# Homes of 1280 bytes at one offset for the moving operands of a float32r GEMM chain

## The chip, the cores and the metric

The kernel runs on one core of one Trainium2 chip. The metric is the device time of one execution in microseconds, as the median of several runs. One execution is also recorded by the hardware profiler; its trace gives the start and length of the instructions on each engine. TensorE multiplies matrices: of a matmul's two operands, one (here 128x128 weights) is loaded into the array first, and the other, the moving operand, is streamed through it. VectorE (DVE), ScalarE (ACT) and GpSimd (POOL) work on elements, SyncE (SP) issues most of the transfers. SBUF is the memory on the core: 128 partitions, in each of which a tile occupies one contiguous stretch of bytes. "Home" stands below for such a stretch, an address in every partition that is the same for all of them.

## What is computed

One step of a hybrid decoder layer over 256 prompt tokens and 8 sample tokens, which the kernel treats as 264 columns. All sums are in float32.

```python
hx = rmsnorm(x, norm_mix)
proj = hx @ w_in                       # 2048 -> 11264
hc, bg, cg, q, fz, iv, og, ga, gb = split(proj)
a = bg * causal_conv3(cg * hc)         # short convolution branch
o, s_new = hgrn2(silu(q), 1 - f, iv, log f)      # 8 heads of 128, gated recurrence
o = rmsnorm(o, onorm_g) * silu(og)
mix = sigmoid(ga) * (a @ w_branch_a) + sigmoid(gb) * (o @ w_branch_b)
x = x + mix @ w_out
h2 = rmsnorm(x, norm_ffn)
x = x + square(relu(h2 @ w_up)) @ w_down         # 2048 -> 8192 -> 2048
y = rmsnorm(x, norm_final)
```

Outputs are y for both kinds of tokens and the new states of the convolution and the recurrence.

## The kernel before

Activations lie transposed: features in the partitions, the 264 tokens along them. A matrix of 2048 features is 16 tiles of 128x264, each 264 x 4 = 1056 bytes per partition. One GEMM makes 128 output features: it walks over 16 blocks k of 128 input features and adds up in one PSUM bank.

To keep float32's precision, each operand is split in two float32r parts, hi (the value rounded to float32r) and lo (the rest). `split` (L58) does it with a cast on ACT (L59) and a subtraction on DVE (L60). `gemm` (L84) then issues three matmuls for each k: weights hi with operand hi (L88), weights hi with operand lo (L89), weights lo with operand hi (L90). So a GEMM of 16 blocks is 48 matmuls of 128x264, and the moving operand changes hi, lo, hi within a block and steps to the next pair of homes for the next block.

Weights come in blocks of 1 MB (`fetch_w`, L65) through SP's queue into `wraw` (two buffers, four once `wraw2` is there), are split in halves (`split_w`, L72) into `whi` and `wlo` of 4096 bytes, four buffers each, and are read 512 bytes at a time.

The stages, in order:

1. Head (`hd`, L157 to L187). Four output blocks are computed together while x and the first weights arrive. For each k, the scaled x is split into `xgh` and `xgl` (L164, L165), which stay for all later GEMMs on x. Each pair (weights part, x part) is streamed against four weight blocks in turn (L179).
2. Projections and recurrence (L484 to L527), an order written out by hand: one weight block for each of 56 slots, GEMM `proj` on the `xg` tiles, the result scaled by `rstd1` out of PSUM. The heads' recurrence (`hgrn`, steps s0 to s14 in successive slots) and the convolution run on the other engines beside it, with small matmuls between GEMMs. Step s3 (L294) makes `kin`, s5 and s6 read it on TensorE; s8 (L367) makes `o`, which s9 to s12 read. The results are split into `oh`, `ol` (L403) and `ah`, `al` (L433), the branch operands.
3. Gates and branches (L542 to L562): for each of 16 output blocks, two gate GEMMs `proj` (fewer at the start) and two GEMMs `br..a`, `br..o` of 8 blocks on the branch operands; the mix is split into `mxh`, `mxl`.
4. `wo` (L567 to L587): 16 GEMMs on the `mx` tiles. The result plus x goes to `x2t` (L574), 4 tiles of four blocks; scaled and split, `x2h` and `x2l` take over the homes of the `xg` tiles.
5. Four quarters of `up` (16 GEMMs on `x2h`, `x2l`) and `dn` (16 GEMMs on `hh`, `hl`, which take the homes of the `mx` tiles), L592 to L630.
6. The end (L633 to L652): the last norm, five multiplications and six transfers of y. After that TensorE runs a probe (L644 to L652): 42 matmuls with float32r operands of 128 to 512 columns out of the last `whi` tile, and 6 in bf16, into a PSUM bank that nobody reads.

Memory comes from pools that are stacked from one end of SBUF: `const`, `wraw`, `wsp`, `act`, `tmp`, then, one after the other in the same place, `xp` and `hp` of the early stages, and `mx`, `x2p`, `wraw2` of the later ones. `act` holds 64 homes of 1056 bytes, 32 for the `xg` and 32 for the `ao` tag (branch operands); `mx` holds 32. In a stack of such homes every next one starts 1056 = 4 x 256 + 32 bytes further. A tag's homes are reused when their last reader is done; a later tile waits for that. Outside the two blocks in a hand-made order (L484 and L633), a scheduler orders the instructions and keeps these waits.

Of the kernel before, what the change touches and what calls it, by code (L numbers as in the profile page):

```python
# [8 lines left out]
F32 = mybir.dt.float32  # L9
F32R = mybir.dt.float32r  # L10
U32 = mybir.dt.uint32
BF16 = mybir.dt.bfloat16
AF = mybir.ActivationFunctionType
ALU = mybir.AluOpType
AX = mybir.AxisListType
# [25 lines left out]
def hybrid_step(ctx: ExitStack, tc: tile.TileContext, x, par, sconv, shg, w_hd, w_in, w_br, w_out, w_up, w_dn,  # L41
# [8 lines left out]
    wraw = ctx.enter_context(tc.tile_pool(name="wraw", bufs=2))  # L50
    wsp = ctx.enter_context(tc.tile_pool(name="wsp", bufs=4))
    act = ctx.enter_context(tc.tile_pool(name="act", bufs=32))
    tmp = ctx.enter_context(tc.tile_pool(name="tmp", bufs=9))
    acc = ctx.enter_context(tc.tile_pool(name="acc", bufs=5, space=PS))
    mps = ctx.enter_context(tc.tile_pool(name="mps", bufs=3, space=PS))
    dram = ctx.enter_context(tc.tile_pool(name="dram", bufs=1, space=bass.MemoryType.DRAM))

    def split(src, hi, lo):  # L58
        nc.scalar.copy(hi, src)  # L59
        nc.vector.tensor_tensor(lo, src, hi.bitcast(F32), op=ALU.subtract)  # L60

    raws = [wraw]
    last_hi = []

    def fetch_w(src):  # L65
        pool = raws.pop(0)
# [5 lines left out]
    def split_w(w, h):  # L72

        hi = wsp.tile([P, 8, P], F32R, tag="hi", name="whi")
        lo = wsp.tile([P, 8, P], F32R, tag="lo", name="wlo")
        split(w[:, h * 1024:(h + 1) * 1024].rearrange("p (k c) -> p k c", c=P), hi, lo)
        last_hi.append(hi)
        return [(hi[:, k], lo[:, k]) for k in range(8)]

    def load_w(src):  # L80
# [55 lines left out]

    pt = const.tile([P, N_PAR], F32, name="pt")
    xg = []
    ss1 = const.tile([P, T], F32, name="ss1")
    p0 = ExitStack()  # L140
    xp = p0.enter_context(tc.tile_pool(name="xp", bufs=1))
    xsq = xp.tile([P, 4, T], F32, name="xsq")
# [14 lines left out]
    for g in range(4):  # L157
        xt, w = xts[g], wts[g]
        whi = [wsp.tile([P, 2, 512], F32R, tag="hi", name="whi") for _ in range(2)]
        wlo = [wsp.tile([P, 2, 512], F32R, tag="lo", name="wlo") for _ in range(2)]  # L160
        for j in range(4):
            k = 4 * g + j
            gk = pt[:, C_NMIX + k:C_NMIX + k + 1]
            hi = act.tile([P, T], F32R, tag="xg", name=f"xgh{k}")  # L164
            lo = act.tile([P, T], F32R, tag="xg", name=f"xgl{k}")  # L165
            wh, wl = whi[j // 2][:, j % 2], wlo[j // 2][:, j % 2]
            if g == 0:
                (nc.vector.tensor_copy if k == 0 else nc.scalar.copy)(wh, w[:, j])
                nc.scalar.activation(hi, xt[:, j], AF.Copy, scale=gk)
                nc.vector.tensor_tensor(wl, w[:, j], wh.bitcast(F32), op=ALU.subtract)  # L170
            else:
                if j % 2 == 0:
                    split(w[:, j:j + 2], whi[j // 2], wlo[j // 2])
                nc.scalar.activation(hi, xt[:, j], AF.Copy, scale=gk)
            nc.vector.scalar_tensor_tensor(lo, xt[:, j], gk, hi.bitcast(F32), op0=ALU.mult, op1=ALU.subtract)
            xg.append((hi, lo))
            for a, b, st, sp in ((wh, hi, k == 0, False), (wl, hi, False, False), (wh, lo, False, k == NK - 1)):
                for i in range(4):
                    nc.tensor.matmul(hps[i], a[:, i * P:(i + 1) * P], b, start=st, stop=sp)  # L179
        if g == 0:  # L180
            nc.scalar.activation(xsq, xt, AF.Square)
        else:
            sq = xp.tile([P, 4, T], F32, tag="xsq2", name="sq", bufs=2)
            nc.scalar.activation(sq, xt, AF.Square)
            nc.vector.tensor_tensor(xsq, xsq, sq, op=ALU.add)
# [14 lines left out]
    nc.gpsimd.memset(smask.rearrange("p a (n l) -> p (a n) l", l=CH)[:, :, 0:1], 0.0)  # L200


    rstd1 = const.tile([P, T], F32, name="rstd1")
    ao = {}
    hctx = ExitStack()
    hp = hctx.enter_context(tc.tile_pool(name="hp", bufs=1))
# [16 lines left out]
    def hgrn(j, q, fz, iv, og):  # L223
# [61 lines left out]
        def s3():  # L285
            for i in range(2):
                fb = hp.tile([P, TS, P], F32, tag="fb", name="fb", bufs=2)
                qb = hp.tile([P, TS, P], F32, tag="qb", name="qb", bufs=2)
                so = hp.tile([P, TS, P], F32, tag="so", name="so", bufs=2)
                nc.sync.dma_start(so, shg[2 * j + i])  # L290
                nc.sync.dma_start(fb, st["scr"][0, i].partition_broadcast(P))
                nc.sync.dma_start(qb, st["scr"][1, i].partition_broadcast(P))
                st["s", i] = fb, qb, so
            st["eb"], st["kin"] = pair_tile("eb", w=TP), pair_tile("kin", w=TP)  # L294
            nc.scalar.activation(st["kend"], st["kend"], AF.Exp)
            nc.scalar.activation(st["kin"], st["b"], AF.Exp, scale=-1.0)
            nc.scalar.activation(st["eb"], st["b"], AF.Exp)
# [66 lines left out]
                                     start=False, stop=(n == 3))  # L364

        def s8():
            o = st["o"] = pair_tile("o")  # L367
            for i in range(2):
                nc.scalar.copy(o[:, i, :TP], st["ops", i][:, :TP])
            s_out(0)  # L370
            for i in range(2):
                nc.sync.dma_start(nhg_p[2 * j + i], st["S", i][:, 3])
# [27 lines left out]

        def s14():
            for i in range(2):
                hi = act.tile([P, T], F32R, tag="ao", name="oh")  # L403
                lo = act.tile([P, T], F32R, tag="ao", name="ol")
                split(og[:, i], hi, lo)
                ao["o", 2 * j + i] = (hi, lo)

# [22 lines left out]
        return a  # L430

    def conv_split(c, a):
        hi = act.tile([P, T], F32R, tag="ao", name="ah")  # L433
        lo = act.tile([P, T], F32R, tag="ao", name="al")
        split(a, hi, lo)
        ao["a", c] = (hi, lo)

# [98 lines left out]


    mx = ctx.enter_context(tc.tile_pool(name="mx", bufs=32))
    x2p = ctx.enter_context(tc.tile_pool(name="x2p", bufs=1))
    raws.append(ctx.enter_context(tc.tile_pool(name="wraw2", bufs=2)))  # L540
    x2t = [x2p.tile([P, 4, T], F32, name=f"x2t{g}") for g in range(4)]
    mix = []  # L542
    for m in range(NK):
        sg = []
        for base in (GA, GB):
            if m < 2:
                t = gate0.pop(0)
            else:
                t = t264("gate")
                proj(base + m, t)  # L550
            nc.scalar.activation(t, t, AF.Sigmoid)
            sg.append(t)
        wk = load_w(w_br[m])
        for i, n in enumerate(("a", "o")):
            ps = acc_tile(f"br{m}{n}")
            gemm(ps, wk[8 * i:8 * i + 8], [ao[n, c] for c in range(8)])
            nc.vector.tensor_tensor(sg[i], sg[i], ps, op=ALU.mult)
        nc.vector.tensor_tensor(sg[0], sg[0], sg[1], op=ALU.add)
        hi = mx.tile([P, T], F32R, tag="mx", name="mxh")
        lo = mx.tile([P, T], F32R, tag="mx", name="mxl")  # L560
        split(sg[0], hi, lo)
        mix.append((hi, lo))  # L562


    x2, x2g = [], []
    ss2 = const.tile([P, T], F32, name="ss2")
    for m in range(NK):  # L567
        xr = t264("xr")
        nc.sync.dma_start(xr, x[:, m, :])
# [3 lines left out]
        t = x2t[m // 4][:, m % 4]  # L573
        nc.vector.tensor_tensor(t, ps, xr, op=ALU.add)  # L574
        gk = pt[:, C_NFFN + m:C_NFFN + m + 1]
        hi = act.tile([P, T], F32R, tag="xg", name="x2h")
        lo = act.tile([P, T], F32R, tag="xg", name="x2l")
        nc.scalar.activation(hi, t, AF.Copy, scale=gk)
        nc.vector.scalar_tensor_tensor(lo, t, gk, hi.bitcast(F32), op0=ALU.mult, op1=ALU.subtract)
        if m == 0:  # L580
# [6 lines left out]
        x2g.append((hi, lo))  # L587


    ss3 = const.tile([P, T], F32, name="ss3")  # L590
    rstd2 = None
    for qd in range(NQ):  # L592
        hh = []
        for m in range(NK):
            wk = load_w(w_up[qd * NK + m])
            ps = acc_tile("up")
            gemm(ps, wk, x2g)
            if rstd2 is None:
                ps2 = mps.tile([P, 512], F32, tag="m", name="ps2")
                sumsq(ps2, ss2, True, True)  # L600
                rstd2 = const.tile([P, T], F32, name="rstd2")
                nc.scalar.copy(rstd2, rstd_bcast(rstd_diag(ps2, 2048, "rstd2"), "rstd2"))
            t = t264("h")
            nc.vector.scalar_tensor_tensor(t, ps, 0.0, rstd2, op0=ALU.max, op1=ALU.mult)
            nc.scalar.activation(t, t, AF.Square)
            hi = mx.tile([P, T], F32R, tag="mx", name="hh")
            lo = mx.tile([P, T], F32R, tag="mx", name="hl")
            split(t, hi, lo)
            hh.append((hi, lo))
        for m in range(NK):  # L610
# [22 lines left out]
    with tc.manual_schedule():  # L633
# [6 lines left out]
        nc.vector.scalar_tensor_tensor(x2[-1], x2[-1], pt[:, C_NFIN + 15:C_NFIN + 16], bps,  # L640
                                       op0=ALU.mult, op1=ALU.mult)
        nc.sync.dma_start(y[:, 15:16, :], x2t[3][:, 3:4])

        probe = acc.tile([P, 512], F32, tag="acc", name="probe")  # L644
        mv = last_hi[-1]
        row = mv.rearrange("p k c -> p (k c)")
        for n in (512, 128, 256, 264, 280, 320, 384):
            for k in range(6):
                nc.tensor.matmul(probe[:, :n], mv[:, k], row[:, :n], start=True, stop=True)  # L649
        half_w = row.bitcast(BF16)  # L650
        for k in range(6):
            nc.tensor.matmul(probe[:, :T], half_w[:, k * P:(k + 1) * P], half_w[:, :T], start=True, stop=True)  # L652


# [53 lines left out]
```

## Time and profile before

| | us |
|---|---|
| median of 3 runs | 1501.76 (1501.73 to 1501.98) |
| profiled execution | 1501.61 |
| its span, first to last instruction | 1499.9 |
| first `proj` matmul | 32.9 |
| first branch matmul | 387.1 |
| first `wo` matmul | 643.5 |
| first `up` matmul | 737.2 |
| last `dn` matmul | 1486.5 |

The first three rows come from the times, the others from the trace, in microseconds from the start of the span. The granted TensorE clock was 0.999 of full speed over the span. A page of the profile gives, for each group of instructions, line, engine, operation, output and inputs by the program's names, the count, busy time, mean duration, and idle time ahead of it with what ended it. The views of a tile give, for each line, minimum, median and maximum duration in ns, and first and last start. A row of the timeline gives start, length, engine, line and count; several instructions in a row that are alike are merged. Durations of matmuls overlap, so their distance is read from starts.

### The profile page before, as it was taken

To read this page: it belongs to the slowest core of one execution; us is meant where nothing else is said; L and a number is where in the kernel's file an instruction comes from. 1 tells how busy PE (TensorE), PEld (TensorE's weight loads), DVE (VectorE), ACT (ScalarE), POOL (GpSimd) and SP (SyncE) were. 2 spreads that over 40 slices of the span, in tenths; PEclk is the share of its full clock that TensorE was granted. 3 is DMA by queue.
4 is the path that set the end of the run, shared out by engine and by line. 5 is a ranking of instruction groups with operands and counts; after the bars stand their busy time and mean duration, and the time that the engine had idled before them with its cause. 6 is when DMAs were issued, how large, how long until landed. Compare 5 with 4: busy or idle time off the path is not lost.

```text
span 1499.9 us, 28243 instructions
## 1 busy us (share of the span) xinstructions
PE 1492.7 (100%) x12230; PEld 1487.2 (99%) x12230; DVE 884.8 (59%) x1154; ACT 705.8 (47%) x946; POOL 57.6 (4%) x86
## 2 busy tenths in 40 slices
PE   9999999999999999999999999999999999999999
PEld 8999999999999999999999999999999999999998
DVE  7576777777655555566655545555455554455554
ACT  6556565646444444444454433444334433344542
POOL 0001011012000000001100000000000000000000
PEclk9999999999999999999999999999999999999999
DMA  6565756665655454555545555454554545545441
GB/s 258 185 256 184 263 189 237 211 241 203 243 176 190 172 192 171 186 202 196 206 170 182 184 172 192 171 186 180 174 192 170 191 173 180 186 171 193 171 169 59
DMA packets 47501, 285.91 MB, mean 191 GB/s; under 512 B 5472, under 2 KB 9328, under 8 KB 16144
## 3 DMA queue, kind: packets, MB, share of 16 engines
q1 hardware_dynamic: 46560, 283.38, 53.0%
q8 instruction: 95, 1.56, 0.4%
q10 hardware_dynamic: 720, 0.59, 0.1%
q14 instruction: 30, 0.25, 0.0%
q0 software_dynamic: 96, 0.14, 0.0%
HBM read 277.07 MB, written 7.02 MB: 189 GB/s over the span
## 4 chain that ended last, share of the span: by engine, by line
PE 98%; DVE 1%; DMA 1%; ACT 0%; issue 0%; ACTq 0%
PE proj L88 11%; PE proj L89 11%; PE proj L90 10%; PE dn L88 8%; PE dn L90 8%; PE up L88 8%; PE dn L89 8%; PE up L89 8%; PE up L90 8%; PE wo L89 2%; PE wo L90 2%; PE wo L88 2%; PE hd L179 1%; PE probe L649 1%; DMA wt<-in_w_hd_dram 0%; PE dlps L332 0%
## 5 line engine op out<-in xcount | busy, mean ns | idle before, releaser
L59 ACT CAST whi<-w 128x1024 fp32r<-128x1024 f32 x488 | 509.5, 1050 | 696.8 <-PE dn L89 218.6
L60 DVE TENSOR_TENSOR wlo<-w,whi 128x1024 fp32r<-128x1024 f32 x488 | 597.8, 1234 | 371.3 <-ACT whi L59 369.5
L88 PE MATMUL proj<-xgh,whi 128*128 128x264 f32 x1344 | 383.5, 285 | 0.4 <-DVE q L462 0.4
L90 PE MATMUL proj<-xgh,wlo 128*128 128x264 f32 x1344 | 381.9, 284 | 0.0
L89 PE MATMUL proj<-xgl,whi 128*128 128x264 f32 x1344 | 380.9, 283 | 0.0
L88 PE MATMUL dn<-hh,whi 128*128 128x264 f32 x1024 | 292.7, 286 | 0.0
L90 PE MATMUL dn<-hh,wlo 128*128 128x264 f32 x1024 | 291.6, 285 | 0.0
L89 PE MATMUL dn<-hl,whi 128*128 128x264 f32 x1024 | 291.4, 285 | 0.0
L89 PE MATMUL up<-x2l,whi 128*128 128x264 f32 x1024 | 291.2, 284 | 0.0
L88 PE MATMUL up<-x2h,whi 128*128 128x264 f32 x1024 | 290.8, 284 | 0.0
L90 PE MATMUL up<-x2h,wlo 128*128 128x264 f32 x1024 | 289.7, 283 | 0.0
L88 PEld LDWEIGHTS proj<-xgh,whi 128*128 128x128 f32 x1344 | 253.4, 189 | 1.7 <-ACT whi L59 0.5
L89 PEld LDWEIGHTS proj<-xgl,whi 128*128 128x128 f32 x1344 | 253.4, 189 | 0.2
L90 PEld LDWEIGHTS proj<-xgh,wlo 128*128 128x128 f32 x1344 | 252.3, 188 | 0.0
L90 PEld LDWEIGHTS dn<-hh,wlo 128*128 128x128 f32 x1024 | 193.5, 189 | 0.0
L90 PEld LDWEIGHTS up<-x2h,wlo 128*128 128x128 f32 x1024 | 193.4, 189 | 0.0
L89 PEld LDWEIGHTS dn<-hl,whi 128*128 128x128 f32 x1024 | 193.4, 189 | 0.0
L88 PEld LDWEIGHTS dn<-hh,whi 128*128 128x128 f32 x1024 | 192.4, 188 | 0.0
L89 PEld LDWEIGHTS up<-x2l,whi 128*128 128x128 f32 x1024 | 192.2, 188 | 0.0
L88 PEld LDWEIGHTS up<-x2h,whi 128*128 128x128 f32 x1024 | 192.1, 188 | 0.0
L90 PE MATMUL wo<-mxh,wlo 128*128 128x264 f32 x256 | 73.0, 285 | 0.0
L89 PE MATMUL wo<-mxl,whi 128*128 128x264 f32 x256 | 72.9, 285 | 0.0
(398 smaller groups left out, 1326.6 us busy)
## 6 DMA issues: line engine op xcount, KB each, us to landing
w<-in_w_in_dram SPq DMA_DIRECT2D x84, 1024.0 KB, 4.8
w<-in_w_up_dram SPq DMA_DIRECT2D x64, 1024.0 KB, 4.8
w<-in_w_dn_dram SPq DMA_DIRECT2D x64, 1024.0 KB, 4.7
w<-in_w_br_dram SPq DMA_DIRECT2D x16, 1024.0 KB, 4.8
w<-in_w_out_dram SPq DMA_DIRECT2D x16, 1024.0 KB, 4.8
so<-in_shg_dram SPq DMA_DIRECT2D x8, 512.0 KB, 7.5
fb<-scr SPq DMA_DIRECT2D x8, 512.0 KB, 8.4
qb<-scr SPq DMA_DIRECT2D x8, 512.0 KB, 10.0
```

The source lines that it names most:

```text
L59: nc.scalar.copy(hi, src)
L60: nc.vector.tensor_tensor(lo, src, hi.bitcast(F32), op=ALU.subtract)
L88: nc.tensor.matmul(ps, wh, xh, start=(k == 0), stop=False)
L89: nc.tensor.matmul(ps, wh, xl, start=False, stop=False)
L90: nc.tensor.matmul(ps, wl, xh, start=False, stop=(k == n - 1))
L179: nc.tensor.matmul(hps[i], a[:, i * P:(i + 1) * P], b, start=st, stop=sp)
L649: nc.tensor.matmul(probe[:, :n], mv[:, k], row[:, :n], start=True, stop=True)
```

## The change

It does seven things:

- The operands `xgh`/`xgl`, `mxh`/`mxl`, `x2h`/`x2l` and `hh`/`hl` get homes of 320 words (1280 bytes), of which they use the last 264 words (`part`). A home's data starts 224 bytes into it.
- Two tiles that nobody reads or writes, `pad_const` (96 bytes) and `pad_tmp` (224 bytes), shift what is stacked behind them.
- The branch operands move from `act` into a pool of their own, `aop`, at the other end of SBUF, still 32 homes of 1056 bytes; it is closed after the last branch GEMM.
- `x2t` is allocated after that, behind `wraw2`, instead of ahead of it.
- `ss1`, `ss2` and `ss3` share one home, `rstd1` and `rstd2` another.
- `kin` is allocated 264 wide and used 256 wide, and `o` takes the same home.
- The probe at the end is gone.

```diff
     act = ctx.enter_context(tc.tile_pool(name="act", bufs=32))
+    actx = ExitStack()
+    aop = actx.enter_context(tc.tile_pool(name="aop", bufs=32, side="right"))
     tmp = ctx.enter_context(tc.tile_pool(name="tmp", bufs=9))
...
+    def part(pool, tag, name):
+
+        return pool.tile([P, 320], F32R, tag=tag, name=name)[:, 320 - T:]
+
...
+    const.tile([P, 24], F32, name="pad_const")
+    tmp.tile([P, 56], F32, tag="pad", name="pad_tmp", bufs=1)
     raws = [wraw]
-    last_hi = []
...
-    ss1 = const.tile([P, T], F32, name="ss1")
+    ss1 = const.tile([P, T], F32, tag="ss", name="ss1")
...
-            hi = act.tile([P, T], F32R, tag="xg", name=f"xgh{k}")
-            lo = act.tile([P, T], F32R, tag="xg", name=f"xgl{k}")
+            hi = part(act, "xg", f"xgh{k}")
+            lo = part(act, "xg", f"xgl{k}")
...
-            st["eb"], st["kin"] = pair_tile("eb", w=TP), pair_tile("kin", w=TP)
+            st["eb"], st["kin"] = pair_tile("eb", w=TP), pair_tile("kin")[:, :, :TP]
...
-            o = st["o"] = pair_tile("o")
+            o = st["o"] = pair_tile("o", tag="kin")
...
-                hi = act.tile([P, T], F32R, tag="ao", name="oh")
-                lo = act.tile([P, T], F32R, tag="ao", name="ol")
+                hi = aop.tile([P, T], F32R, tag="ao", name="oh")
+                lo = aop.tile([P, T], F32R, tag="ao", name="ol")
...
     mx = ctx.enter_context(tc.tile_pool(name="mx", bufs=32))
-    x2p = ctx.enter_context(tc.tile_pool(name="x2p", bufs=1))
     raws.append(ctx.enter_context(tc.tile_pool(name="wraw2", bufs=2)))
-    x2t = [x2p.tile([P, 4, T], F32, name=f"x2t{g}") for g in range(4)]
...
-        hi = mx.tile([P, T], F32R, tag="mx", name="mxh")
-        lo = mx.tile([P, T], F32R, tag="mx", name="mxl")
+        hi = part(mx, "mx", "mxh")
+        lo = part(mx, "mx", "mxl")
...
+    actx.close()
+    x2p = ctx.enter_context(tc.tile_pool(name="x2p", bufs=1))
+    x2t = [x2p.tile([P, 4, T], F32, name=f"x2t{g}") for g in range(4)]
...
-        probe = acc.tile([P, 512], F32, tag="acc", name="probe")
-        mv = last_hi[-1]
-        row = mv.rearrange("p k c -> p (k c)")
-        for n in (512, 128, 256, 264, 280, 320, 384):
-            for k in range(6):
-                nc.tensor.matmul(probe[:, :n], mv[:, k], row[:, :n], start=True, stop=True)
-        half_w = row.bitcast(BF16)
-        for k in range(6):
-            nc.tensor.matmul(probe[:, :T], half_w[:, k * P:(k + 1) * P], half_w[:, :T], start=True, stop=True)
```

`ah`/`al`, `x2h`/`x2l`, `hh`/`hl`, `ss2`, `ss3` and `rstd2` change in the same way as the lines shown.

More of the change, by code (lines that the diff above doesn't have):

```diff
@@ L11 @@
 U32 = mybir.dt.uint32
-BF16 = mybir.dt.bfloat16
 AF = mybir.ActivationFunctionType
@@ L76, in split_w @@
         split(w[:, h * 1024:(h + 1) * 1024].rearrange("p (k c) -> p k c", c=P), hi, lo)
-        last_hi.append(hi)
         return [(hi[:, k], lo[:, k]) for k in range(8)]
@@ L200, in hybrid_step @@
     nc.gpsimd.memset(smask.rearrange("p a (n l) -> p (a n) l", l=CH)[:, :, 0:1], 0.0)
-    rstd1 = const.tile([P, T], F32, name="rstd1")
+    rstd1 = const.tile([P, T], F32, tag="rstd", name="rstd1")
     ao = {}
@@ L432, in conv_split @@
     def conv_split(c, a):
-        hi = act.tile([P, T], F32R, tag="ao", name="ah")
-        lo = act.tile([P, T], F32R, tag="ao", name="al")
+        hi = aop.tile([P, T], F32R, tag="ao", name="ah")
+        lo = aop.tile([P, T], F32R, tag="ao", name="al")
         split(a, hi, lo)
@@ L558, in hybrid_step @@
         nc.vector.tensor_tensor(sg[0], sg[0], sg[1], op=ALU.add)
-        hi = mx.tile([P, T], F32R, tag="mx", name="mxh")
-        lo = mx.tile([P, T], F32R, tag="mx", name="mxl")
+        hi = part(mx, "mx", "mxh")
+        lo = part(mx, "mx", "mxl")
         split(sg[0], hi, lo)
         mix.append((hi, lo))
+    actx.close()
+    x2p = ctx.enter_context(tc.tile_pool(name="x2p", bufs=1))
+    x2t = [x2p.tile([P, 4, T], F32, name=f"x2t{g}") for g in range(4)]
     x2, x2g = [], []
-    ss2 = const.tile([P, T], F32, name="ss2")
+    ss2 = const.tile([P, T], F32, tag="ss", name="ss2")
     for m in range(NK):
@@ L575, in hybrid_step @@
         gk = pt[:, C_NFFN + m:C_NFFN + m + 1]
-        hi = act.tile([P, T], F32R, tag="xg", name="x2h")
-        lo = act.tile([P, T], F32R, tag="xg", name="x2l")
+        hi = part(act, "xg", "x2h")
+        lo = part(act, "xg", "x2l")
         nc.scalar.activation(hi, t, AF.Copy, scale=gk)
@@ L587, in hybrid_step @@
         x2g.append((hi, lo))
-    ss3 = const.tile([P, T], F32, name="ss3")
+    ss3 = const.tile([P, T], F32, tag="ss", name="ss3")
     rstd2 = None
@@ L600, in hybrid_step @@
                 sumsq(ps2, ss2, True, True)
-                rstd2 = const.tile([P, T], F32, name="rstd2")
+                rstd2 = const.tile([P, T], F32, tag="rstd", name="rstd2")
                 nc.scalar.copy(rstd2, rstd_bcast(rstd_diag(ps2, 2048, "rstd2"), "rstd2"))
@@ L605, in hybrid_step @@
             nc.scalar.activation(t, t, AF.Square)
-            hi = mx.tile([P, T], F32R, tag="mx", name="hh")
-            lo = mx.tile([P, T], F32R, tag="mx", name="hl")
+            hi = part(mx, "mx", "hh")
+            lo = part(mx, "mx", "hl")
             split(t, hi, lo)
```

## The prediction

> **What bounds the kernel now.** I read the page first: busy times, granted clock, and the chain that ended last.
>
> ```profile
> span 1499.9 us, 28243 instructions
> ...
> PE 1492.7 (100%) x12230; PEld 1487.2 (99%) x12230; DVE 884.8 (59%) x1154; ACT 705.8 (47%) x946; POOL 57.6 (4%) x86
> ...
> PEclk9999999999999999999999999999999999999999
> ...
> PE 98%; DVE 1%; DMA 1%; ACT 0%; issue 0%; ACTq 0%
> ...
> L88 PE MATMUL proj<-xgh,whi 128*128 128x264 f32 x1344 | 383.5, 285 | 0.4 <-DVE q L462 0.4
> ...
> L88 PE MATMUL dn<-hh,whi 128*128 128x264 f32 x1024 | 292.7, 286 | 0.0
> ...
> L88 PE MATMUL up<-x2h,whi 128*128 128x264 f32 x1024 | 290.8, 284 | 0.0
> ```
>
> TensorE is on the chain for 98% of the span at full clock and waits for nobody in its large groups. No load can be hidden better. Only the spacing of matmuls can change, and that isn't the mean of 285 ns (matmuls overlap) but the distance between starts. The views of a tile, by window, give the first and last start of each line; a line starts every third matmul. For `proj`, interleaved with the recurrence, I take two rows of the timeline around one pair of gates.
>
> ```profile
> L88 PE MATMUL wo<-mxh,whi x256: 279/283/288, 643.5 to 736.8; 128*128 128x264 f32 x128
> ...
> L88 PE MATMUL dn<-hh,whi x256: 280/288/291, 831.4 to 924.9; 128*128 128x264 f32 x128
> ...
> L88 PE MATMUL up<-x2h,whi x256: 279/284/289, 925.3 to 1018.1; 128*128 128x264 f32 x128
> ...
> L88 PE MATMUL dn<-hh,whi x256: 279/283/288, 1018.5 to 1111.8; 128*128 128x264 f32 x128
> ...
> 398.72 0.29 PE L88 MATMUL proj<-xgh,whi 128*128 128x264 f32 x1
> ...
> 410.37 0.28 PE L88 MATMUL br2a<-ah,whi 128*128 128x264 f32 x1
> ```
>
> Between 256 starts of a line lie 765 matmuls: `wo` 93.3 us, 121.96 ns each; `up` 92.8, 121.31; `dn` 93.5 in its first quarter, 122.22, and 93.3 in its second, 121.96 (mean 122.09). The gate pair is 96 matmuls in 11.65 us, 121.35. One instruction form, five spacings; the two `dn` quarters differ by nothing but the order in which their operands lie in memory (median of the line 288 against 283 ns). That is what the change touches.
>
> How far down could it go? Three rows of the probe at the end (its moving operand is always the start of one weight tile), with their means:
>
> ```profile
> 1494.89 0.52 PE L649 MATMUL probe<-whi 128*128 128x264 f32 x3
> ...
> 1496.89 1.03 PE L649 MATMUL probe<-whi 128*128 128x384 f32 x5
> ...
> 1497.94 0.85 PE L652 MATMUL probe<-whi 128*128 128x264 bf16 x6
> ...
> L649 PE MATMUL probe<-whi 128*128 128x384 f32 x6 | 1.2, 336 | 0.0
> ...
> L649 PE MATMUL probe<-whi 128*128 128x264 f32 x6 | 0.9, 282 | 0.0
> L652 PE MATMUL probe<-whi 128*128 128x264 bf16 x6 | 0.9, 278 | 0.0
> ```
>
> A row's length less one duration, over the gaps in it, is the spacing: 264 columns (0.52-0.282)/2 = 119 ns, 384 columns (1.03-0.336)/4 = 173.5, and bf16 (0.85-0.278)/5 = 114. At 384 columns one column costs 0.452 ns, so 264 cost 119.3: about 119 to 120 is the rate of streaming four-byte operands, and the kernel's 121.3 to 122.1 lie 1 to 2% above it.
>
> The head stage shows what the place does. There each `xgh`/`xgl` is streamed 8 and 4 times running.
>
> ```profile
> 26.70 0.65 PE L179 MATMUL hd<-xgh,whi 128*128 128x264 f32 x4
> ...
> 27.66 0.64 PE L179 MATMUL hd<-xgl,whi 128*128 128x264 f32 x4
> 28.14 0.64 PE L179 MATMUL hd<-xgh,whi 128*128 128x264 f32 x4
> ...
> 29.60 0.65 PE L179 MATMUL hd<-xgh,whi 128*128 128x264 f32 x4
> ...
> 31.07 0.64 PE L179 MATMUL hd<-xgh,whi 128*128 128x264 f32 x4
> ...
> 32.51 0.56 PE L114 MATMUL ps<-ones,ss 128*88 128x1 f32 x6
> ```
>
> Four k of 12 matmuls each: 1.44, 1.46, 1.47, 1.44 us, so 120.0, 121.7, 122.5 and 120.0 ns. In the memory map of before these operands (k = 12 to 15) start at 0/224, 192/160, 128/96 and 64/32 past a multiple of 256: a home of 1056 bytes is 4 x 256 + 32, so homes in a row run through eight offsets. The `xgl` block of k = 12 lies at 224, the new common offset: 0.48 us for four, 120.
>
> **The change part by part.** *Homes.* The new map adds up as follows. `const` loses three homes of 1056 by sharing and gains 96, so `wraw` starts at 24576; 16384 and 32768 later `act` starts at 73728, and after 40960 there and 9728 of `tmp` (with its pad of 224), `mx` at 124416. All are multiples of 256, 1280 is too, and data begins 224 into its home: every moving operand of `proj`, `wo`, `up` and `dn` starts at 224 and ends on a multiple of 256. The instructions stay the same. Unknown is the spacing when every operand follows one at the same offset; no gemm of before has that. Bounds from rows: 119.3 (the 384-column row) and 122.5 (k = 14). I take 120.0, the nearest rows being the `xgl` block at 224 and the 264-column probe, which repeats one place. Gains: `proj` 84 x 48 = 4032 matmuls x 1.35 = 5.4 us; `up` 3072 x 1.31 = 4.0; `dn` 3072 x 2.09 = 6.4; `wo` 768 x 1.96 = 1.5. Sum 17.3 us, all on the chain. The branch gemms (768) keep unpadded homes at the other end: 0, within 1 us either way.
>
> [...]
>
> *Probe.* It holds TensorE for 1497.94+0.85-1489.98 = 8.8 us, but not the end:
>
> ```profile
> 1489.98 8.12 PE L649 MATMUL probe<-whi 128*128 128x512 f32 x42
> 1490.37 4.54 DVE L638 TENSOR_TENSOR x2t<-x2t,bps_rstd 128x528 f32<-128x528 f32 x5 [0.87 <-PE bps_rstd L131]
> ...
> 1495.40 0.48 SPq L642 DMA_DIRECT2D out_dram<-x2t  x1
> ...
> out_dram<-x2t SPq DMA_DIRECT2D x1, 132.0 KB, 2.9
> ```
>
> The last output is issued at 1495.40 and lands 2.9 us later, at 1498.3; the probe ends at 1498.8, the span at 1499.9. Without the probe the end follows the output: 0 to 0.5 us, I take 0.3.
>
> *Moves and shared homes.* `o` in `kin`'s home and `x2t` over the branch operands add waits.
>
> ```profile
> L296 ACT ACTIVATE kin<-b x4: 613/614/617, 77.9 to 307.5; 128x512 f32<-128x512 f32 x4
> ...
> L396 DVE TENSOR_TENSOR og<-og,o x4: 702/702/705, 136.6 to 367.2; 128x528 f32<-128x528 f32 x4
> ...
> L90 PE MATMUL br15o<-oh,wlo x8: 279/284/288, 640.9 to 643.4; 128*128 128x264 f32 x8
> ...
> L574 DVE TENSOR_TENSOR x2t<-wo,xr x16: 432/433/434, 649.6 to 737.4; 128x264 f32<-128x264 f32 x16
> ```
>
> `kin` of the next pair is written (307.5-77.9)/3 = 76.5 us after the first, at 154.4; the last reader of `o` starts at 136.6 and takes 0.7: 17 us spare. Were they short, ACT would stand with the weight casts queued behind and TensorE behind those. `x2t` is first written at 649.6, six us after the last branch read at 643.4. If it had to wait, DVE would hold back the next weight split behind it, and TensorE after that. Both cost 0. `ss` and `rstd` of different stages lie further apart still. The moved `wraw2` is loaded by the same SP queue in the same order. No DMA is added. At 17 us less, DVE's 884.8 and ACT's 705.8 are still under 60% of the span: nothing else becomes late.
>
> **Sum.** 1499.9 - 17.3 - 0.3 = 1482.3. The profiled execution took 1501.61, 1.7 more than its span, which makes 1484.0; the median of the runs, 1501.76, is 0.15 above that execution: **1484.2**. One ns of spacing is worth 10.9 us (10,944 matmuls); spacings of 119.5 to 120.7 make 1478.7 to 1491.9.
>
> **Rivals.**
> 1. *Half of it:* 121.04, the mean of the four head k (5.81 us over 48), as hi and lo homes still differ by 1280, and each is followed by another weight tile. For it: even repeats of one operand reach 122.5. Against: offsets 0 and 224 are the quiet ones. Gain 10.944 x (121.59-121.04) = 6.0, with the tail 1495.5. (121.59 is the mean of the four stages, weighted by count.)
> 2. *The place does nothing:* the differences come from what else runs, or from weight loads, whose tiles keep their offsets. Against: the two `dn` quarters. Only the tail is left, 1501.5. [...]
> 3. *Slower, locked in a bad phase:* with eight offsets, good and bad successions average out; with one, every matmul meets the same one. Place: the gemms; price: k = 14's 122.5 everywhere, (122.5-121.59) x 10.944 = 10.0 us, 1511.5. It decides from 121.6 on. For it: at 128/96 a constant place was slow. Against: at 224 it wasn't.
> 4. *Better than my floor:* 119.3 everywhere, 1476.5.
>
> **How the numbers follow.** Forecast 0.58, half 0.17, nothing 0.11, locked slow 0.10, better 0.04. The range takes the forecast and the half case and leaves out most of the others: 1478 to 1499. About 0.2% (3 us) is what a measurement here can tell from no change. Faster by more: forecast, half and better, 0.79; within: 0.11; slower: 0.10.
>
> **What would show it.** Right: in the changed profile the same rows of `wo`, `up` and both `dn` quarters give about 120.0, alike in all, and the branch rows stay as they are; the end follows the last output by about 1 us. Wrong: stages that still differ from each other (place isn't it), or that agree at 121.6 or more (locked), or a new idle time ahead of TensorE released by DVE `x2t` or ACT `kin`.

## The result and the profile after

The kernel after took 1484.39 us (median of 4 runs, 1484.05 to 1485.0) beside 1501.74 (1500.99 to 1501.98) for the kernel before in the same session: ratio 0.9885, 95% interval 0.9872 to 0.9897. The profiled execution took 1484.52 us.

The page of the profile after; the lines of `gemm` that were L88 to L90 are L94 to L96 now:

```profile
span 1482.8 us, 28147 instructions
...
PE 1467.2 (99%) x12182; PEld 1462.4 (99%) x12182; DVE 884.5 (60%) x1154; ACT 705.8 (48%) x946; POOL 57.5 (4%) x86
...
PE 97%; DVE 1%; DMA 1%; ACT 0%; issue 0%; DVEq 0%; ACTq 0%
...
L94 PE MATMUL proj<-xgh,whi 128*128 128x264 f32 x1344 | 382.5, 285 | 0.4 <-DVE q L468 0.4
...
L94 PE MATMUL up<-x2h,whi 128*128 128x264 f32 x1024 | 289.1, 282 | 0.0
L94 PE MATMUL dn<-hh,whi 128*128 128x264 f32 x1024 | 288.9, 282 | 0.0
```

TensorE is still 97% of the chain and its large groups still wait for nobody: no new idle time from `x2t` or `kin` appears. The mean length of a `proj` matmul is the same 285 ns as before, so durations alone hardly show the change. Two windows of the profile after, the GEMMs and the end (busy time and count of each engine, then granted clock, DMA share, GB/s), say whether the clock did it:

```profile
33.00:1466.00 1433.00, 1432.36 (x11925) 1429.34 (x11924) 854.53 (x1107) 683.63 (x911) 54.08 (x70) 1.00 0.54 192
1466.00:1482.00 16.00, 5.08 (x42) 4.40 (x40) 6.12 (x10) 0.63 (x2) 0.00 (x0) 0.74 0.34 135
```

It did not: TensorE was granted its full clock throughout the GEMMs, as before; the 0.74 belongs to the last 16 us, with 42 matmuls in them. In the same 1433 us the kernel before gets fewer matmuls through:

```profile
33.00:1466.00 1433.00, 1432.48 (x11786) 1429.44 (x11786) 847.58 (x1098) 677.20 (x902) 54.13 (x70) 1.00 0.54 192
```

11,925 against 11,786, in the same busy time. So each follows the one ahead of it sooner. The views of the tiles after, with first and last start, and the timeline's two rows around the same gate pair as before. The tiles:

```profile
L94 PE MATMUL wo<-mxh,whi x256: 280/282/287, 638.7 to 730.5; 128*128 128x264 f32 x128
...
L94 PE MATMUL dn<-hh,whi x256: 280/282/283, 824.0 to 915.8; 128*128 128x264 f32 x128
...
L94 PE MATMUL up<-x2h,whi x256: 280/282/283, 916.1 to 1007.9; 128*128 128x264 f32 x128
...
L94 PE MATMUL dn<-hh,whi x256: 280/282/283, 1008.3 to 1100.1; 128*128 128x264 f32 x128
```

The timeline:

```profile
395.67 0.29 PE L94 MATMUL proj<-xgh,whi 128*128 128x264 f32 x1
...
407.19 0.28 PE L94 MATMUL br2a<-ah,whi 128*128 128x264 f32 x1
```

Four times 91.8 us over 765 gaps, and 11.52 us over 96: 120.0 ns each time. Before they were 121.96, 122.22, 121.31, 121.96 and 121.35. The two `dn` quarters no longer differ, and the spread of a line's lengths shrank from 11 ns (280 to 291) to 3. The end:

```profile
1473.34 4.54 DVE L645 TENSOR_TENSOR x2t<-x2t,bps_rstd 128x528 f32<-128x528 f32 x5 [0.87 <-PE bps_rstd L137]
...
1478.37 0.41 SPq L649 DMA_DIRECT2D out_dram<-x2t  x1
```

The last multiplications begin at 1473.34 instead of 1490.37, 17.03 us earlier. Of that, `wo` begins 4.8 us earlier (638.7 against 643.5), `wo` itself saves 1.5, and the rest, 10.7, lies in `up` and `dn`. Behind the last output's issue the span runs 4.43 us on, against 1499.9 - 1495.40 = 4.50 before.

### The profile page after: what moved, and what is told of

Its sections match the earlier page's. It is cut to its first block, busy times and chain, and to the rows that moved or that the text cites. A ratio compares the mean times of both kernels' runs of the same rounds, so it can differ in the third digit from the quotient of the medians.

```text
span 1482.8 us, 28147 instructions
## 1 busy us (share of the span) xinstructions
PE 1467.2 (99%) x12182; PEld 1462.4 (99%) x12182; DVE 884.5 (60%) x1154; ACT 705.8 (48%) x946; POOL 57.5 (4%) x86
## 4 chain that ended last, share of the span: by engine, by line
PE 97%; DVE 1%; DMA 1%; ACT 0%; issue 0%; DVEq 0%; ACTq 0%
PE proj L94 11%; PE proj L96 11%; PE proj L95 11%; PE dn L94 8%; PE up L94 8%; PE up L95 8%; PE dn L95 8%; PE up L96 8%; PE dn L96 8%; PE wo L95 2%; PE wo L94 2%; PE wo L96 2%; PE hd L185 1%; DMA wt<-in_w_hd_dram 0%; PE dlps L338 0%; PE ops L369 0%
## 5 line engine op out<-in xcount | busy, mean ns | idle before, releaser
L94 PE MATMUL proj<-xgh,whi 128*128 128x264 f32 x1344 | 382.5, 285 | 0.4 <-DVE q L468 0.4
L96 PE MATMUL proj<-xgh,wlo 128*128 128x264 f32 x1344 | 379.5, 282 | 0.0
L94 PE MATMUL up<-x2h,whi 128*128 128x264 f32 x1024 | 289.1, 282 | 0.0
L94 PE MATMUL dn<-hh,whi 128*128 128x264 f32 x1024 | 288.9, 282 | 0.0
L96 PE MATMUL up<-x2h,wlo 128*128 128x264 f32 x1024 | 288.9, 282 | 0.0
L96 PE MATMUL dn<-hh,wlo 128*128 128x264 f32 x1024 | 288.9, 282 | 0.0
L94 PEld LDWEIGHTS proj<-xgh,whi 128*128 128x128 f32 x1344 | 252.1, 188 | 1.7 <-ACT whi L64 0.6
L96 PEld LDWEIGHTS proj<-xgh,wlo 128*128 128x128 f32 x1344 | 252.1, 188 | 0.0
L94 PEld LDWEIGHTS up<-x2h,whi 128*128 128x128 f32 x1024 | 191.9, 187 | 0.0
L94 PEld LDWEIGHTS dn<-hh,whi 128*128 128x128 f32 x1024 | 191.9, 187 | 0.0
L96 PEld LDWEIGHTS dn<-hh,wlo 128*128 128x128 f32 x1024 | 191.9, 187 | 0.0
L96 PEld LDWEIGHTS up<-x2h,wlo 128*128 128x128 f32 x1024 | 191.9, 187 | 0.0
L94 PE MATMUL wo<-mxh,whi 128*128 128x264 f32 x256 | 72.2, 282 | 0.0
```

Of the source, the lines that this page charges most:

```text
L94: nc.tensor.matmul(ps, wh, xh, start=(k == 0), stop=False)
L96: nc.tensor.matmul(ps, wl, xh, start=False, stop=(k == n - 1))
```

## Experiments

**What the theories were.** The prediction's: it matters at which offset the moving operand lies, and that every operand follows one at the same offset. Rivals: that only this one place is good; that the weights' place matters as well; that the moves and shared homes gave the gain; that accesses of the other engines set the pace. Expectations are quoted as they stood ahead of each run. A GEMM's spacing is taken from its starts; where no row stands beside it, I took it from all starts of the stage in the trace.

### Parts of the change that give nothing: the probe

The kernel before without its probe:

```diff
-        probe = acc.tile([P, 512], F32, tag="acc", name="probe")
...
-                nc.tensor.matmul(probe[:, :n], mv[:, k], row[:, :n], start=True, stop=True)
...
```

> The kernel before without the 48 matmuls of the probe at its end, homes as they were. Theory (the end waits for the last output, not for the probe): 0.0 to 0.5 us faster, 1501.3 to 1501.7; from the two profiles, where the end follows the issue of the last output by 4.50 us before and 4.43 after, rather 0.1 than 0.3. Rival (the probe holds the end): 8.8 us faster, 1493.

1501.58 us (1501.01 to 1502.23, 10 runs) beside 1501.9; ratio 0.9998, interval 0.9989 to 1.0008. The timeline's last issue of an output:

```profile
1495.57 0.48 SPq L642 DMA_DIRECT2D out_dram<-x2t  x1
```

From there to the end of the span (1500.1) are 4.53 us, as with the probe. The 8.8 us of matmuls lay beside the last multiplications and the last output's way to memory, and cost nothing that these runs can tell.

### The moves without the homes, and a pad alone

First the kernel after, with the old homes of 1056 bytes:

```diff
 def part(pool, tag, name):
-    return pool.tile([P, 320], F32R, tag=tag, name=name)[:, 320 - T:]
+    return pool.tile([P, T], F32R, tag=tag, name=name)
```

> The changed kernel with homes of 1056 bytes again, all else of the change kept (no probe, branch operands at the other end, x2 later, shared homes). Theory (the common offset gives all of the gain): 1501 to 1502.5, with up, dn and wo at 121.3 to 122.2 ns a matmul again. Rival (the moves or shared homes give part of it): below 1498.

1498.18 us (1497.87 to 1498.52), ratio 0.9976, interval 0.9967 to 0.9985. My expectation missed by 3 us: some of the gain came without the padded homes. By the starts it lay in `dn` and `wo` (121.25 and 121.14 ns, before 122.07 and 121.96); `proj` and `up` stayed within 0.03. That pointed to where the `mx` homes begin, which by the pools' sizes is now a multiple of 256 and was 32 past one. So: the kernel before, with no move and no shared home, but with 224 unused bytes ahead of `mx` (and no probe, which costs nothing).

```diff
+    tmp.tile([P, 56], F32, tag="pad", name="pad_tmp", bufs=1)
```

> The kernel before without its probe, with one pad of 224 bytes ahead of the later pools, so that the mx homes (1056 bytes, as before) start at a multiple of 256 instead of 32 past it. Nothing else is changed. Theory (the 3.7 us of the run with 1056-byte homes came from this shift): wo and dn at 121.1 to 121.4, proj and up as before, 1498.2 within 1 us. Rival (they came from the moves or the shared homes): 1501.6.

1498.31 us (1497.73 to 1498.57, 10 runs), ratio 0.9977, interval 0.9968 to 0.9986: the same. The view of the tile `wo`:

```profile
L89 PE MATMUL wo<-mxh,whi x256: 278/283/289, 643.3 to 735.9; 128*128 128x264 f32 x128
```

92.6 us, 121.05 ns. One pad is worth 3.2 us (the kernel before: 1501.5 in that session); what the moves and shared homes add to it (0.9976 against 0.9977) is nothing that these runs can tell. The other 13.8 us of the change, from 1498.18 to 1484.39 in two sessions, come with the homes of 1280 bytes alone. Why the succession of eight offsets is better from this start was not tried.

### The same homes with another offset

Each of these is the kernel after with data at another place in the home of 1280 bytes, the same place for all:

```diff
-        return pool.tile([P, 320], F32R, tag=tag, name=name)[:, 320 - T:]
+        return pool.tile([P, 320], F32R, tag=tag, name=name)[:, :T]
```

This is offset 0; `32:32 + T` makes 128 bytes, `8:8 + T` makes 32.

> The changed kernel with the data at the start of each home, so every moving operand of the large GEMMs starts on a multiple of 256 and none ends there. Theory (what counts is that a matmul's operand follows one at the same offset): 1484.4 within 1 us, 120.0 ns a matmul. Rival (the end on a multiple of 256, offset 224, is what helps): between, above 1490, 120.6 ns or more.

1489.15 us (1488.58 to 1489.34), ratio 0.9916 (0.9901 to 0.9931). It has two spacings:

```profile
L94 PE MATMUL wo<-mxh,whi x256: 278/283/289, 642.1 to 734.9; 128*128 128x264 f32 x128
...
L94 PE MATMUL dn<-hh,whi x512: 280/281/282, 828.4 to 1104.6; 128*128 128x264 f32 x171
```

`wo` took 92.8 us for 765 gaps, 121.3 ns, with lengths from 278 to 289; `dn` has lengths within 2 ns of each other, and its starts give 120.0. Same offset, same instruction, two steady paces, and a time that neither the theory nor the rival had named. By this view `dn` keeps its pace from the first start to the last, 512 starts of a line in two quarters with a quarter of `up` between them. What let the pace change between `wo` and `dn` is not shown.

> The changed kernel with the data 128 bytes into each home. Theory of the common offset: 1484.4 within 1 us, 120.0 ns. Rival (some offsets are bad in themselves; in the head stage of before the k at offsets 128 and 96 had 122.5 ns): 122 to 123.5 ns everywhere, 1506 to 1523, slower than the kernel before.

1488.64 us (1486.78 to 1489.41), ratio 0.9911 (0.9896 to 0.9926). One `proj` GEMM by two rows of the timeline, then `wo` by the view of its tile:

```profile
51.64 0.29 PE L94 MATMUL proj<-xgh,whi 128*128 128x264 f32 x1
...
57.56 0.29 PE L94 MATMUL proj<-xgh,whi 128*128 128x264 f32 x1
```

```profile
L94 PE MATMUL wo<-mxh,whi x256: 283/284/287, 643.1 to 734.9; 128*128 128x264 f32 x128
```

That GEMM took 5.92 us for 48 matmuls, 123.3 ns; `wo` 91.8, 120.0. Again two paces, the slow one slower, and again neither forecast: not 120.0 throughout, and not slower than the kernel before.

> The changed kernel with its common offset at 32 instead of 224. From the sweep, where offset 32 settled at 122.22 ns from all six leads: (122.2 - 121.6) x 10.9 = 7 us slower than the kernel before, 1508 to 1509. Rival (a common offset is good as such, and the slow states of the sweep are made by its leads): 1484.4 to 1490.

1508.43 us (1508.12 to 1509.11), ratio 1.0046 (1.0031 to 1.0061): slower than before, though every operand follows one at the same offset.

```profile
L94 PE MATMUL up<-x2h,whi x256: 280/282/282, 929.5 to 1023.0; 128*128 128x264 f32 x128
```

93.5 us over 765 gaps, 122.2 ns, and by the starts 122.1 to 122.3 in every stage. This is the prediction's third rival, "locked in a bad phase", at another offset.

Then two offsets instead of one: the hi parts at 224, the lo parts at 96.

```diff
-        return pool.tile([P, 320], F32R, tag=tag, name=name)[:, 320 - T:]
+        at = 56 if name.rstrip("0123456789")[-1] == "h" else 24
+        return pool.tile([P, 320], F32R, tag=tag, name=name)[:, at:at + T]
```

> The changed kernel with all hi operands at offset 224 and all lo operands at 96: the pattern still repeats with every k, but neighbours no longer share an offset. Theory (a matmul is at 120 ns when it follows one at the same offset): 120.8 to 122.5 ns, 1493 to 1511. Rival (a pattern that repeats is enough): 120.0 ns, 1484.4 within 1 us.

1509.66 us (1509.45 to 1510.13), ratio 1.0053 (1.0038 to 1.0068).

```profile
L95 PE MATMUL dn<-hh,whi x256: 286/286/286, 1024.8 to 1118.3; 128*128 128x264 f32 x128
```

Again 122.2 ns, with not one ns between shortest and longest: a lock, and a slow one. Two thirds of the matmuls are where they were in the kernel after.

### The spacing by itself

Behind the last output of the kernel after, groups of 32 matmuls of 264 columns read one `wlo` tile at offset 0, 32, ... 224 against the weights of one `whi` tile. Both tiles begin on multiples of 256. Ahead of each group one matmul of 300, 314, ... 370 columns (`lead0` to `lead5`) shifts the time at which it starts.

```diff
+        def sweep(name, offs, n=T, count=32, lead=None):
...
+            if lead:
+                nc.tensor.matmul(ps[:, :lead], wt[:, 0], row[:, :lead], start=True, stop=True)
+            for i in range(count):
+                o = offs[i % len(offs)] // 4
+                nc.tensor.matmul(ps[:, :n], wt[:, i % 8], row[:, o:o + n], start=True, stop=True)
```

> The changed kernel, and after its last output some 2,000 matmuls more into a bank that nobody reads: runs of 32 matmuls of 264 columns at one offset, for eight offsets, each started after a lead matmul of 300 to 370 columns (six leads, so six phases); runs at offsets 4 and 16; runs that step by 32; and 256 to 512 columns at offsets 0 and 224. Some 300 us longer for that. Theory (one offset has a few steady states, which the phase at the start chooses, and 224 has only the fast one): six times 120.0 at 224; 120.0 or about 121.4 at 0; 120.0 or about 123.3 at 128; steps of 32 at 121 to 122.5. Rival (224 has a slow state too, and the kernel's pauses happened to miss it): one or more of the six at 224 above 121. [...]

A single execution, 1791.33 us with the added matmuls. First a window of it (columns as in the windows above: us, then PE, PEld, DVE, ACT and POOL, granted clock, DMA share, GB/s):

```profile
1500.00:1600.00 100.00, 100.00 (x813) 100.00 (x812) 0.00 (x0) 0.00 (x0) 0.00 (x0) 1.00 0.00 1
```

Nothing but TensorE works in this window, at full clock (1.00), so paces that differ within it come neither from other engines nor from the clock. Rows of the timeline, each one group:

```profile
1507.30 4.07 PE L662 MATMUL at32lead0x<-wlo,whi 128*128 128x264 f32 x32
...
1564.12 4.21 PE L662 MATMUL at96lead2x<-wlo,whi 128*128 128x264 f32 x32
...
1572.53 4.05 PE L662 MATMUL at96lead4x<-wlo,whi 128*128 128x264 f32 x32
...
1592.88 4.12 PE L662 MATMUL at128lead3x<-wlo,whi 128*128 128x264 f32 x32
...
1597.00 4.00 PE L662 MATMUL at128lead4x<-wlo,whi 128*128 128x264 f32 x32
...
1653.47 4.00 PE L662 MATMUL at224lead0x<-wlo,whi 128*128 128x264 f32 x32
...
1673.47 4.01 PE L662 MATMUL at224lead5x<-wlo,whi 128*128 128x264 f32 x32
...
1724.00 3.99 PE L662 MATMUL at0cols256x<-wlo,whi 128*128 128x256 f32 x32
...
1748.90 7.46 PE L662 MATMUL at0cols512x<-wlo,whi 128*128 128x512 f32 x32
1756.20 3.95 PE L662 MATMUL at224cols256x<-wlo,whi 128*128 128x256 f32 x32
...
1781.04 7.62 PE L662 MATMUL at224cols512x<-wlo,whi 128*128 128x512 f32 x32
```

A row's length less one matmul's (0.28 us), over 31 gaps, is the spacing, to about 0.3 ns. Offset 224: 120.0 to 120.3 after every lead. Offset 32: 121.9 to 122.3. Offset 96: 126.7 once settled after five leads, and 121.6 after one. Offset 128: 120.0 or about 123.5 (123.3 once settled). Taken from the starts, offsets 0 and 64 also have two paces each (120.0, and 121.2 or 120.95), and 160 one (121.7); 192 begins slower but is at 120.0 in its last 16 matmuls after all six leads. Between the leads little but the time of the start differs, so in this sweep it is the start that chooses among an offset's paces (at 96, 126.7 or 121.6). A group that steps up through the eight offsets took 120.7 ns a matmul, just under the 121 to 122.5 expected, and one that steps down 122.1.

The last four rows bear on the floor. At offset 0, 256 columns take (3.99-0.28)/31 = 119.7 ns, as long as 264 within 0.3; by the prediction's 0.452 ns a column they should take 115.7. 512 columns, by their starts, take 228 where that rate gives 231. So at offset 0 the time is no plain rate of columns. At offset 224 it is nearer to one: by the starts 118.3 ns for 256 columns, 120.0 for 264 and 233 for 512, which are 0.462, 0.455 and 0.455 ns a column.

A second sweep takes the multiples of 8 bytes that were missing, with four leads, and bf16 (`T` columns, weights in bf16 too) at four offsets:

```diff
-        for o in range(0, 256, 32):
-            for j in range(6):
+        for o in range(8, 256, 16):
+            for j in range(4):
...
+        for o in range(16, 256, 32):
+            for j in range(4):
```

> As the first sweep, at odd multiples of 8 and of 16, four leads each, and in bf16 at offsets 0, 32, 96 and 224. Some 340 us longer. Theory (120.0 is the best of the steady states, not a property of offset 224): no offset under 119.9 over a run, several at 120.0, several at 121 to 127. Rival (finer offsets hold something better): a run settled under 119.5. [...]

A single execution, 1892.64 us with the added matmuls.

```profile
1604.07 4.15 PE L662 MATMUL at120lead1x<-wlo,whi 128*128 128x264 f32 x32
...
1747.12 4.00 PE L662 MATMUL at16lead0x<-wlo,whi 128*128 128x264 f32 x32
...
1878.98 3.77 PE L675 MATMUL half32x<-wlo,whi 128*128 128x264 bf16 x32
...
1886.18 3.77 PE L675 MATMUL half224x<-wlo,whi 128*128 128x264 bf16 x32
```

120 bytes gives 124.8 ns, 16 bytes 120.0, and bf16 (3.77-0.28)/31 = 112.6 at each of its four offsets, with one group each. In both sweeps no group of 264 four-byte columns settled more than 0.2 ns below 120.0. Those at 16, 144, 176 and 208 settled at 120.0 after all four leads, so 224 isn't alone. The bf16 groups show no dependence on the offset.

### Is it the operand's place, or its distance from the weights?

In the kernel after, `whi` and `wlo` begin on multiples of 256. Here they are moved by 128 bytes, and nothing else moves by anything but multiples of 256:

```diff
+    wpad = ctx.enter_context(tc.tile_pool(name="wpad", bufs=1))
...
+    wpad2 = ctx.enter_context(tc.tile_pool(name="wpad2", bufs=1))
...
+    wpad.tile([P, 32], F32, name="pad_w")
+    wpad2.tile([P, 32], F32, name="pad_w2")
```

> The changed kernel with the weights' homes shifted by 128 bytes (a pad ahead of them and one behind), moving operands still at 224. Theory A (what counts is the moving operand's offset alone): 1484.4 within 1 us. Theory B (what counts is its distance to the weights, which are read at the same time: 96 now instead of 224): slow states as at other offsets, 120.4 ns or more in some stages, 1487 to 1500.

1502.04 us (1501.43 to 1503.77, 10 runs), ratio 1.0004 (0.9994 to 1.0013): the whole gain is gone, with the moving operands still at 224, and 2 us more than the theory's range. Two `proj` GEMMs by the timeline, then two lines of tile views:

```profile
51.70 0.28 PE L98 MATMUL proj<-xgh,whi 128*128 128x264 f32 x1
...
57.54 0.28 PE L98 MATMUL proj<-xgh,whi 128*128 128x264 f32 x1
...
209.94 0.29 PE L98 MATMUL proj<-xgh,whi 128*128 128x264 f32 x1
...
216.02 0.29 PE L98 MATMUL proj<-xgh,whi 128*128 128x264 f32 x1
```

```profile
L98 PE MATMUL wo<-mxh,whi x256: 280/285/287, 654.6 to 747.7; 128*128 128x264 f32 x128
...
L98 PE MATMUL dn<-hh,whi x256: 284/284/284, 1025.7 to 1117.5; 128*128 128x264 f32 x128
```

48 matmuls in 5.84 and 6.08 us: 121.7 and 126.7 ns. These are the two paces of offset 96 in the sweep, and 224 - 128 = 96. `wo` runs at 121.7; `up` and `dn` found a pace of 120.0, which six leads at 96 did not show. So the time of the kernel before returns by other means: `proj`, at a mean of 123.8 ns by its starts, is slower than it was there (121.2), while `up` and `dn` keep their gain.

Now the data is moved along with the weights, to 96 bytes into its home, so that the distance is 224 again (96 - 128 + 256):

```diff
-        return pool.tile([P, 320], F32R, tag=tag, name=name)[:, 320 - T:]
+        return pool.tile([P, 320], F32R, tag=tag, name=name)[:, 24:24 + T]
```

> Weights' homes shifted by 128 bytes, and the data in the moving operands' homes too, to offset 96, which with the weights unshifted ran at 126.7 or 121.6 ns. The distance from weights to moving operand, modulo 256, is 224 as in the changed kernel. Theory B (the distance counts): 120.0 ns, 1484.4 within 1 us. Theory A' (each address counts for itself, both the weights' and the operand's): 121.6 to 126.7, 1502 or more.

1485.07 us (1484.76 to 1485.78), ratio 0.9891 (0.9875 to 0.9908): the gain is back.

```profile
L98 PE MATMUL wo<-mxh,whi x256: 280/282/283, 638.9 to 730.7; 128*128 128x264 f32 x128
```

120.0 ns, here and in `proj`, `up` and `dn`. At the two distances tried, 96 and 224, what counts is the distance from the weights to the moving operand, modulo 256, and not the address of either.

### The branches too

The kernel after, with the branch operands in such homes as well. Room for it comes from four more shared homes in the recurrence (`kk` with `vk0`, `kend` with `vk1`, `sig` with `S0`, `b` with `S1`).

```diff
+    apad = actx.enter_context(tc.tile_pool(name="apad", bufs=1, side="right"))
+    apad.tile([P, 56], F32, name="pad_a")
...
-                hi = aop.tile([P, T], F32R, tag="ao", name="oh")
-                lo = aop.tile([P, T], F32R, tag="ao", name="ol")
+                hi = part(aop, "ao", "oh")
+                lo = part(aop, "ao", "ol")
```

> The changed kernel with the branch operands in homes of 1280 at offset 224 as well (a pad of 224 at the other end; room from four shared homes in the recurrence). Theory: the branch GEMMs go from 121.6 to 120.0, 768 matmuls x 1.58 = 1.2 us, 1483.2. Rival (the short GEMMs of 8 blocks don't settle, or the shared homes add a wait): 1484.4 or more.

1483.28 us (1482.94 to 1483.52), ratio 0.9876 (0.9862 to 0.9891), 1.1 us under the kernel after: the fastest version here. A pair of branch GEMMs, 48 matmuls, by the timeline of the kernel after and then of this one:

```profile
389.82 0.29 PE L94 MATMUL br1a<-ah,whi 128*128 128x264 f32 x1
```

```profile
389.46 0.28 PE L96 MATMUL br1a<-ah,whi 128*128 128x264 f32 x1
...
395.22 0.28 PE L96 MATMUL proj<-xgh,whi 128*128 128x264 f32 x1
```

The kernel after needs 395.67 - 389.82 = 5.85 us, 121.9 ns; this one 5.76, 120.0.

## Why the prediction held, and where its reasons did not

**The sum was right.** 1484.2 was forecast. Up to the last multiplications 17.3 us were forecast and 17.03 came. By terms: `wo` 1.5 as forecast, `up` and `dn` 10.4 against 10.7, `proj` 5.4 against at most 4.8. `proj` was over-sized because it rests on one gate pair at 121.35 ns; the mean over the stage was 121.22 before and 120.04 after, and 4032 x 1.18 is 4.8. `up` was taken from one quarter (121.31), while the mean of all four was about 121.4.

**The bounds and the pace.** `wo`, `up` and both `dn` quarters at 120.0 was the forecast's own sign, and it came. The lower bound of the pace, 119.3, rested on 0.452 ns a column taken as a rate; the rows with 256 and 512 columns contradict that rate at offset 0, and at 224 they lie 0.7 to 2.2% above it. The number 120 was right by its nearest rows, the `xgl` block at 224 and the probe; the reason given for it as a floor is not shown.

**The tail** was forecast at 0.3 us and measured 0.07 in the trace; the span ends 1.5 us behind the last output's landing (median 2.9 us after its issue), not about 1. Taking out the probe alone makes no difference within the interval. **Moves and shared homes** at 0: right, since the old homes with the moves give no more than a pad alone. **Branches** unchanged: right within the bound of 1 us; their GEMMs ran at 121.6 ns in both kernels.

**What failed as a reason is "follows one at the same offset".** Offset 32 has that in every GEMM and is slower than the kernel before. It isn't the moving operand's place alone either. The prediction named the weights only in its second rival, where their tiles "keep their offsets"; yet with the weights moved by 128 bytes the gain vanished, and with both moved it returned. The prediction came out because the change's offset, 224, is one at which these runs show only the good pace (120.0 to 120.3 ns after all six leads). The head's `xgl` block, four matmuls, had shown that pace at the same distance; that it would be the only one there was not known, and in so far it was luck. In the third rival, "against: at 224 it wasn't" was the argument that carried; "for it" came true at another offset: 1508.4 us at 32, against 1511.5 worked out.

Rival 2 (place does nothing) falls by all of the offset runs, rivals 1 (half) and 4 (119.3) by the 120.0 of the large stages.

The bf16 groups took 112.6 ns at each of four offsets, the groups of 264 four-byte columns 120.0 to 126.7 once settled. The pace of the moving operand changed when only the weights were moved, from 120.0 to 121.7 and 126.7 in `proj`: that decides that the weights' place matters here, not where the two meet.

**What stays open.** That the reads of weights and moving operand get in each other's way would fit a pace that hangs on their distance, on their relative time at the start, and on four-byte operands; it is argued, not shown. Nor is it known why 32 and 160 showed only a slow pace (122.2 and 121.7 ns) and 0, 64 and 128 a fast one (120.0) beside it, nor what sets the floor of 120.

## What to carry to other kernels

Where TensorE is the chain and never idle, compare the distance between starts in every stage: lengths of matmuls overlap and hide it (here 285 ns for `proj` before and after, with starts 121.2 and 120.0 ns apart). With four-byte operands like these, of 264 columns, lay moving operands and weights at one fixed distance modulo 256 that a sweep over several starting times shows to have the fast pace alone (224 here, 120.0 to 120.3 ns after six leads); a fixed distance as such can lock in a slow one, 0.5% behind the mixed homes here (1508.43 us at 32). A pad of 224 bytes alone was worth 0.2% (1498.31 against 1501.5 us), so in a kernel like this a change that shifts pools can show a gain of this size that has nothing to do with its purpose.

## What I had not expected of the hardware

A stream of equal matmuls at equal offsets ran at two or three steady paces here: 126.7, 121.7 or 120.0 ns with weights and data 96 apart. In the sweep at 96 the start chose between 126.7 and 121.6; with the weights moved, `dn` kept 120.0 over 256 starts of a line, all 284 ns long. At offset 0, 256 and 264 columns of four-byte operands take the same time within 0.3 ns (119.7 and 120.0); at offset 224 they differ by 1.7.
